# Norms and softplus of a two-block transformer kernel: half a square sum on VectorE, epsilon as a column, softplus on VectorE

## Chip, cores and metric

One core of a Trainium2 chip runs the whole program. The metric is the device time of one launch in microseconds (us). The engines are named as in the profile: PE is TensorE (its weight loads are PEld), DVE is VectorE, ACT is ScalarE, POOL is GpSimd, and SP issues the DMAs.

## What is computed

The input is 256 rows of width 1024, all in float32. A first block mixes a stick-breaking attention and a Mamba-2 (SSD) branch, then does a cross attention to a memory and a SwiGLU feed-forward. A second block has two layers: forget-gate attention ("fox") and latent attention ("mla"), each beside a small memory attention and followed by a convolutional feed-forward. Cut to what the change touches:

```
rms_norm(x, g) = x * rsqrt(mean(x*x, axis=-1) + 1e-6) * g        # rows of 1024, also q and k of each head (64 or 96)
dt             = softplus(dt_raw + dt_bias)                       # SSD: 2 x 32 heads per row
log_f          = log_sigmoid(f + b_f) = -softplus(-(f + b_f))     # fox: 12 heads per row
```

## The kernel before

The 256 rows are two tiles of 128 (t = 0 and t = 1), one row per partition. Every weight block of 128 x 1024 comes by DMA into `wr`. It is split into a high part `wh` (a rounding copy, by ACT or DVE) and a low part `wl` (the difference, by DVE or POOL). PE makes three products per block (high by high, low by high, high by low). These products are most of PE's work, and the splits are most of the work of ACT and DVE.

The program is written as some dozens of small generator threads (one per tile, per attention lane, per norm). A planner runs them first without the chip. `Engine` (L327) gives each operation an estimated cost, `Model` (L181 to L309) keeps the estimated time of every engine and buffer, and `next` (L480) picks the thread whose next operation can start first, with priorities and due times. `model_kernel` (L2231) plans once, then up to six times more with the order and the due times of the pass before, and emits the pass whose PE ends first in the model. So the order of every engine's queue comes from the estimated costs, and a changed operation can change the order of all that follows. Where a thread yields a list of operations, as for the copies of the weight split, the planner takes the engine on which it would end first. All operations are emitted through L363, so all have that line in the profile; matmuls have L652 and transposes L656.

The pieces that the change touches:

- `rms` (L828): the sum of squares of a row of 1024, as two halves. ACT squares each half with a running sum into one column (`accum_out`, in the trace an ACTIVATE and an ACTIVATION_READ_ACCUMULATOR), one half after the other, with one scratch of 512 columns. It runs 18 times: for both tiles of x, `mem` and `mem_2` (`inv_rms`, L862), before the cross attention, fox and mla (`prenorm`, L837), and before the three feed-forwards (`prenorm_joint`, L886). In `prenorm_joint` x is scaled by the result before it is transposed, so PE's transposes come after the norm; in `prenorm` the result is only applied to products.
- `rsqrt` (L682): two POOL steps. A TENSOR_SCALAR adds the two halves and epsilon, and a TENSOR_TENSOR raises to the power -1/2 (`mhalf`).
- `headnorm` (L1727): the same for the heads of a row. ACT squares n x d elements, DVE reduces them to n sums, POOL adds epsilon, POOL takes the power, DVE multiplies; then PE transposes the result (`heads_T`, `mem_q`). It runs 18 times: 12 times with 8 heads (fox: d = 64, mla: d = 96, three chunks and two tiles each) and 6 times with 4 heads.
- `softplus` (L995): exp on ACT, then a series in u/(2+u). Three of its steps are on DVE and 19 on POOL. It runs once for SSD's dt (128 x 64, called from `dt_part`, L1285) and once per tile for fox's gate (128 x 12, called from `fox_gate`, L1914). In `fox_gate` a product with a triangle of ones (`triu`) follows, whose result every q and k of that tile waits for.

Of the kernel before, what the change touches and what calls it, by code (L numbers as in the profile page):

```python
# [15 lines left out]
OP = mybir.AluOpType  # L16
AX = mybir.AxisListType.X

D = 1024
# [301 lines left out]
class Engine:  # L321
# [5 lines left out]
    def __getattr__(self, op):  # L327
# [3 lines left out]
        def call(*a, **k):  # L331
# [20 lines left out]
            else:  # L352
                port = bool(ins)
                c = 0.0023 * n + 0.25
                if k.get("op") == OP.pow:
                    c = 0.165 * n + 0.45
                elif op == "affine_select":
                    c = 0.00145 * n + 0.1
                elif op == "tensor_copy":
                    c = 0.001 * n + 0.19  # L360
                elif op == "memset":
                    c = 0.0009 * n + 0.07
# [17 lines left out]
class Program:  # L380
# [300 lines left out]

    def rsqrt(self, r, ms, more=None):  # L682

        n = r.shape[1]
        if more is None:
            yield self.G.tensor_scalar(ms, ms, EPS, None, op0=OP.add)
        else:
            yield self.G.tensor_scalar(ms, ms, more, EPS, op0=OP.add, op1=OP.add)
        yield self.G.tensor_tensor(r, ms, self.const["mhalf"][:, :n], op=OP.pow)

    def drop(self, key, users=2):
# [136 lines left out]
    def rms(self, src, r):  # L828

        junk = yield ("b", 512)  # L830
        m0, m1 = self.col(), self.col()
        for h, m in enumerate((m0, m1)):
            yield self.act(junk.ap, src[:, 512 * h:512 * h + 512], "Square", scale=1.0 / 32, accum_out=m)
        junk.free()
        yield from self.rsqrt(r, m0, m1)

# [117 lines left out]
    def postnorm(self, bs, x, name):  # L954
# [6 lines left out]
        junk.free()  # L961
        yield from self.rsqrt(r, m0, m1)
        y = yield ("b", D)
# [31 lines left out]
    def softplus(self, out, x, n):  # L995

        V, G = self.V, self.G
        w = yield ("b", n * 5)
        a, u, s, s2, q = (w.ap[:, i * n:(i + 1) * n] for i in range(5))
        yield V.scalar_tensor_tensor(a, x, -1.0, x, op0=OP.mult, op1=OP.max)  # L1000
        yield self.act(u, a, "Exp", scale=-1.0)
        yield G.tensor_scalar(s, u, 2.0, None, op0=OP.add)
        yield V.reciprocal(s, s)
        yield G.tensor_tensor(s, s, u, op=OP.mult)
        yield G.tensor_tensor(s2, s, s, op=OP.mult)
        yield G.tensor_scalar(q, s2, 1.0 / 15, None, op0=OP.mult)
        for m in (13, 11, 9, 7, 5, 3):
            yield G.tensor_scalar(q, q, 1.0 / m, None, op0=OP.add)
            yield G.tensor_tensor(q, q, s2, op=OP.mult)
        yield G.tensor_scalar(q, q, 1.0, 2.0, op0=OP.add, op1=OP.mult)  # L1010
        yield G.tensor_tensor(q, q, s, op=OP.mult)
        yield V.tensor_scalar(a, x, 0.0, None, op0=OP.max)
        yield G.tensor_tensor(out, q, a, op=OP.add)
        w.free()
# [712 lines left out]
    def headnorm(self, dst, src, n, d):  # L1727

        yield ("m", [n * d, 2 * n], [])
        junk = yield ("b", n * d)  # L1730
        s = yield ("b", 2 * n)
        ms, r = s.ap[:, :n], s.ap[:, n:2 * n]
        yield self.act(junk.v(n), src, "Square", scale=d ** -0.5)
        yield self.V.tensor_reduce(ms, junk.v(n), axis=AX, op=OP.add)
        junk.free()
        yield self.G.tensor_scalar(ms, ms, EPS, None, op0=OP.add)
        yield self.G.tensor_tensor(r, ms, self.const["mhalf"][:, :n], op=OP.pow)
        yield self.V.tensor_tensor(dst, src, r[:, :, None].to_broadcast([128, n, d]), op=OP.mult)
        s.free()
        yield ("r", dst)  # L1740
# [613 lines left out]
```

## Time and profile before

| | |
|---|---|
| time, median of 3 runs | 1309.0 us (1307.93 to 1310.06) |
| the profiled execution's own time | 1311.11 us |
| its span, first to last instruction | 1309.4 us |
| PE busy | 1281.2 us (98%), 8332 matmuls |
| PEld, DVE, ACT, POOL busy | 1142.1 (87%), 932.4 (71%), 810.7 (62%), 181.2 us (14%) |
| granted PE clock, mean | 0.995 |

The share of busy time is that of one execution. Matmuls overlap in the records, and their ends are modelled. So PE at 98% is no statement of peak speed; it says that there are few moments in which no matmul is under way.

### The profile page before, as it was taken

What the parts mean: (1) busy time and instruction counts of PE and PEld (TensorE: products, weight loads), DVE (VectorE), ACT (ScalarE), POOL (GpSimd) and SP (SyncE); (2) the same over time, 40 slices, a digit from 0 to 9 for tenths busy, and PEclk for the clock granted to TensorE, in tenths of its full rate; (3) what the DMA queues carried; (4) which work ended last, traced back from release to release, by engine and by line L of the source; (5) the groups of instructions that cost most, each with busy time, mean ns of one, the idle gap of its engine ahead of it and who ended that gap; (6) DMA issues with size and microseconds to landing.
All of it is one profiled execution on the core that took longest, in us unless ns stands there. A gap on an engine that the chain in (4) does not pass through costs nothing.

```text
span 1309.4 us, 21881 instructions
## 1 busy us (share of the span) xinstructions
PE 1281.2 (98%) x8332; PEld 1142.1 (87%) x8332; DVE 932.4 (71%) x1519; ACT 810.7 (62%) x1443; POOL 181.2 (14%) x324
## 2 busy tenths in 40 slices
PE   8999999999999999999999999899999999999998
PEld 6998998998888888999997888689999777799997
DVE  5766888988675737655447678788776788786774
ACT  6556678786745647544447656876554777865552
POOL 3053010022010002000004521000000332100000
PEclk9999999999999999999999999899999999999999
DMA  8723543455764715655564433476654333375540
GB/s 301 232 75 116 178 161 110 137 203 180 267 213 136 250 66 177 230 188 180 190 227 130 161 113 129 152 234 223 198 185 133 115 113 112 118 247 189 186 164 33
DMA packets 63322, 221.10 MB, mean 169 GB/s; under 512 B 7536, under 2 KB 7664, under 8 KB 63216
## 3 DMA queue, kind: packets, MB, share of 16 engines
q1 hardware_dynamic: 63216, 219.70, 50.2%
q8 instruction: 65, 1.06, 0.3%
q14 instruction: 41, 0.34, 0.1%
HBM read 218.62 MB, written 1.05 MB: 168 GB/s over the span
## 4 chain that ended last, share of the span: by engine, by line
PE 85%; DVE 6%; ACT 5%; DMA 2%; issue 1%; POOL 1%; SPq 0%; ACTq 0%; DVEq 0%; POOLq 0%
PE pa L652 82%; DVE arena L363 3%; PE pa L656 3%; ACT arena L363 3%; DVE wl L363 2%; DMA wr<-in_w_in 1%; ACT wh L363 1%; ACT L553 1%; DVE arena_r L363 1%; POOL small L363 1%; DMA arena<-in_mem 1%; DMA wr<-in_w_up 0%; ACT arena_r L363 0%; POOL arena L363 0%; SPq L660 0%
## 5 line engine op out<-in xcount | busy, mean ns | idle before, releaser
L363 DVE TENSOR_TENSOR wl<-wr,wh 128x1024 fp32r<-128x1024 f32 (+1 forms) x395 | 472.6, 1212 | 178.4 <-ACT wh L363 172.9
L652 PE MATMUL pa<-wh,arena_r 128*128 128x512 f32 (+2 forms) x1812 | 588.2, 394 | 5.1 <-ACT wh L363 3.4
L363 ACT ACTIVATE wh<-wr 128x1024 fp32r<-128x1024 f32 (+2 forms) x393 | 406.6, 1044 | 268.6 <-PE pa L652 187.3
L652 PE MATMUL pa<-arena_r,wh 128*128 128x256 f32 (+2 forms) x2736 | 495.6, 283 | 0.0
L652 PEld LDWEIGHTS pa<-arena_r,wh 128*128 128x128 f32 (+2 forms) x2736 | 425.8, 190 | 4.6 <-issue 1.1
L652 PEld LDWEIGHTS pa<-wh,arena_r 128*128 128x128 f32 x1812 | 340.9, 189 | 76.1 <-ACT wh L363 4.2
L652 PE MATMUL pa<-arena_r,wl 128*128 128x256 f32 (+2 forms) x1368 | 385.6, 282 | 0.0
L652 PE MATMUL pa<-wl,arena_r 128*128 128x512 f32 (+2 forms) x906 | 352.6, 389 | 2.9 <-DVE wl L363 2.9
L652 PEld LDWEIGHTS pa<-arena_r,wl 128*128 128x128 f32 (+2 forms) x1368 | 260.1, 190 | 0.2
L652 PEld LDWEIGHTS pa<-wl,arena_r 128*128 128x128 f32 x906 | 171.6, 189 | 33.9 <-DVE wl L363 3.9
L363 ACT ACTIVATE arena<-arena 128x512 f32<-128x512 f32 (+6 forms) x130 | 80.3, 628 | 31.1 <-DVE arena L363 27.8
L652 PE MATMUL pa<-arena 128*64 128x128 f32 (+4 forms) x888 | 92.5, 288 | 3.2 <-ACT arena L363 2.4
L652 PEld LDWEIGHTS pa<-arena 128*64 128x64 f32 (+3 forms) x888 | 78.0, 161 | 18.4 <-issue 7.0
L363 ACT ACTIVATE arena<-pa 128x512 f32<-128x512 f32 (+4 forms) x98 | 53.6, 555 | 63.6 <-PE pa L652 38.3
L363 POOL TENSOR_SCALAR small<-small 128x1 f32<-128x1 f32 x38 | 15.2, 401 | 494.6 <-ACT arena L363 342.3
L363 DVE TENSOR_TENSOR arena<-arena 128x512 f32<-128x512 f32 (+4 forms) x117 | 68.2, 601 | 13.3 <-POOL arena L363 5.9
L656 PE MATMUL pa<-ident,arena 128*128 128x128 f32 (+3 forms) x446 | 66.6, 281 | 9.6 <-DVE arena L363 7.0
L363 DVE SCALAR_TENSOR_TENSOR arena<-pa,cols,arena 128x255 f32<-128x255 f32 (+1 forms) x136 | 57.7, 476 | 25.6 <-ACT arena L363 24.3
L656 PEld LDWEIGHTS pa<-ident,arena 128*128 128x128 f32 (+3 forms) x446 | 52.7, 139 | 23.3 <-DVE arena L363 10.4
L363 ACT ACTIVATE arena<-pa,small 128x128 f32<-128x128 f32 (+2 forms) x147 | 55.5, 453 | 24.8 <-PE pa L652 24.1
L363 DVE TENSOR_TENSOR arena<-pa,arena 128x512 f32<-128x512 f32 (+3 forms) x74 | 48.9, 670 | 29.1 <-PE pa L652 24.3
L363 DVE SCALAR_TENSOR_TENSOR arena<-arena,cols 128x128 f32<-128x128 f32 (+3 forms) x152 | 59.0, 422 | 6.6 <-ACT arena L363 4.8
(128 smaller groups left out, 777.1 us busy)
## 6 DMA issues: line engine op xcount, KB each, us to landing
wr<-in_w_up SPq DMA_DIRECT2D x96, 512.0 KB, 4.1
wr<-in_w_in SPq DMA_DIRECT2D x80, 512.0 KB, 4.4
wr<-in_w_gu SPq DMA_DIRECT2D x44, 512.0 KB, 4.2
wr<-in_w_dn SPq DMA_DIRECT2D x44, 512.0 KB, 4.7
wr<-in_w_down SPq DMA_DIRECT2D x22, 512.0 KB, 3.6
wr<-in_w_fox SPq DMA_DIRECT2D x20, 512.0 KB, 3.6
wr<-in_w_br_ssm SPq DMA_DIRECT2D x16, 512.0 KB, 4.2
wr<-in_w_xkv SPq DMA_DIRECT2D x16, 512.0 KB, 3.7
```

The lines of the kernel that those rows point to most:

```text
L363: emit = (lambda: f(*a, **k)) if f else (lambda: None)
L553: self.real.preload_act_table_set(s)
L652: self.T.matmul(out, l, r, start=start, stop=stop, skip_group_check=True)
L656: self.T.transpose(out, in_, self.const["ident"][:k, :k])
```

## The change

- `rms`: the second half of the squares may run on DVE (a scalar_tensor_tensor with a running sum); the planner picks ACT or DVE. Where the arena has room, the two halves write to different scratch columns.
- `rsqrt`: it can leave out the epsilon step; with two halves, they swap their places as operands.
- `headnorm`: POOL first writes epsilon to one more column per head, DVE's reduction sums it in, and POOL's step that added it is gone.
- `softplus`: all steps but exp are on DVE, with add and multiply fused: 15 DVE steps and the exp.
- In the cost estimates a power given as second operation is priced as one; no operation of the kernel has that.

```diff
-    def rsqrt(self, r, ms, more=None):
+    def rsqrt(self, r, ms, more=None, eps=True):
-        if more is None:
+        if more is not None:
+            yield self.G.tensor_scalar(ms, ms, more, EPS, op0=OP.add, op1=OP.add)
+        elif eps:
             yield self.G.tensor_scalar(ms, ms, EPS, None, op0=OP.add)
-        else:
-            yield self.G.tensor_scalar(ms, ms, more, EPS, op0=OP.add, op1=OP.add)
         yield self.G.tensor_tensor(r, ms, self.const["mhalf"][:, :n], op=OP.pow)
+    def sumsq(self, junk, src, m, both=False):
+        o = [self.act(junk, src, "Square", scale=1.0 / 32, accum_out=m)]
+        if both:
+            o.append(self.V.scalar_tensor_tensor(junk, src, 1.0 / 1024, src, op0=OP.mult, op1=OP.mult, accum_out=m))
+        return o
 def rms
-        junk = yield ("b", 512)
+        two = self.mem.fits([D])
+        junk = yield ("b", D if two else 512)
-        for h, m in enumerate((m0, m1)):
-            yield self.act(junk.ap, src[:, 512 * h:512 * h + 512], "Square", scale=1.0 / 32, accum_out=m)
+        yield self.sumsq(junk.ap[:, :512], src[:, :512], m0)
+        yield self.sumsq(junk.ap[:, 512 * two:512 * two + 512], src[:, 512:], m1, True)
-        yield from self.rsqrt(r, m0, m1)
+        yield from self.rsqrt(r, m1, m0)
 def softplus (every G below was or becomes V; w, a, u, s, s2, q as before)
-        yield G.tensor_scalar(s, u, 2.0, None, op0=OP.add)
+        yield V.tensor_scalar(s, u, 2.0, None, op0=OP.add)
         yield V.reciprocal(s, s)
-        yield G.tensor_tensor(s, s, u, op=OP.mult)
-        yield G.tensor_tensor(s2, s, s, op=OP.mult)
-        yield G.tensor_scalar(q, s2, 1.0 / 15, None, op0=OP.mult)
+        yield V.tensor_tensor(s, s, u, op=OP.mult)
+        yield V.tensor_tensor(s2, s, s, op=OP.mult)
+        yield V.tensor_scalar(q, s2, 1.0 / 15, None, op0=OP.mult)
         for m in (13, 11, 9, 7, 5, 3):
-            yield G.tensor_scalar(q, q, 1.0 / m, None, op0=OP.add)
-            yield G.tensor_tensor(q, q, s2, op=OP.mult)
-        yield G.tensor_scalar(q, q, 1.0, 2.0, op0=OP.add, op1=OP.mult)
-        yield G.tensor_tensor(q, q, s, op=OP.mult)
+            yield V.scalar_tensor_tensor(q, q, 1.0 / m, s2, op0=OP.add, op1=OP.mult)
+        yield V.scalar_tensor_tensor(q, q, 1.0, s, op0=OP.add, op1=OP.mult)
         yield V.tensor_scalar(a, x, 0.0, None, op0=OP.max)
-        yield G.tensor_tensor(out, q, a, op=OP.add)
+        yield V.scalar_tensor_tensor(out, q, 2.0, a, op0=OP.mult, op1=OP.add)
 def headnorm
-        yield ("m", [n * d, 2 * n], [])
-        junk = yield ("b", n * d)
+        yield ("m", [n * (d + 1), 2 * n], [])
+        junk = yield ("b", n * (d + 1))
+        sq = junk.v(n)
+        yield self.G.memset(sq[:, :, d:], EPS)
-        yield self.act(junk.v(n), src, "Square", scale=d ** -0.5)
-        yield self.V.tensor_reduce(ms, junk.v(n), axis=AX, op=OP.add)
+        yield self.act(sq[:, :, :d], src, "Square", scale=d ** -0.5)
+        yield self.V.tensor_reduce(ms, sq, axis=AX, op=OP.add)
-        yield self.G.tensor_scalar(ms, ms, EPS, None, op0=OP.add)
-        yield self.G.tensor_tensor(r, ms, self.const["mhalf"][:, :n], op=OP.pow)
+        yield from self.rsqrt(r, ms, eps=False)
```

## Rows read from the trace of the kernel before

**Rows 1.** Busy time by stretch: us, then PE, PEld, DVE, ACT, POOL, clock, DMA.
```profile
60.00:155.00 95.00, 94.97 (x720) 87.19 (x719) 68.35 (x100) 58.90 (x94) 33.41 (x48) 1.00 0.36 120
824.00:850.00 26.00, 21.57 (x89) 17.08 (x88) 22.32 (x47) 23.10 (x44) 1.46 (x6) 0.87 0.54 182
1060.00:1100.00 40.00, 36.98 (x239) 30.18 (x237) 33.27 (x81) 30.20 (x79) 11.10 (x20) 0.96 0.32 106
```
**Rows 2.** Waits of PE: who waited for whom, us in total, times, longest.
```profile
PE pa L656 <- DVE arena L363: 7.0, 7, 3.4
...
PE pa L652 <- POOL small L363: 1.9, 2, 1.2
```
**Rows 3.** Timeline, 705 to 720, fox's softplus of t = 0 on POOL.
```profile
706.65 0.67 POOL L363 TENSOR_SCALAR arena<-arena 128x12 f32<-128x12 f32 x1 [2.42 <-ACT arena L363]
...
709.22 1.11 POOL L363 TENSOR_SCALAR arena<-arena 128x12 f32<-128x12 f32 x1
...
718.00 0.77 POOL L363 TENSOR_TENSOR small<-arena 128x12 f32<-128x12 f32 x1 [0.54 <-DVE arena L363]
```
**Rows 4.** Timeline of PE, 715 to 720.
```profile
718.83 0.39 PE L652 MATMUL pa<-small,triu 128*128 128x12 f32 x2 [1.20 <-POOL small L363]
```
**Rows 5.** DVE's groups by shape: busy us, mean ns, idle before.
```profile
L363 DVE SCALAR_TENSOR_TENSOR arena<-pa,small,arena 128x512 f32<-128x512 f32 x24 | 17.5, 743 | 16.1 <-POOL small L363 13.3 <-PE pa L652 2.7
...
L363 DVE TENSOR_REDUCE arena<-arena 128x128 f32<-128x512 f32 x8 | 8.5, 1083 | 1.0 <-ACT arena L363 0.9
...
L363 DVE TENSOR_SCALAR arena<-arena 128x12 f32<-128x12 f32 x4 | 0.7, 172 | 0.1
...
L363 DVE RECIPROCAL arena<-arena 128x12 f32<-128x12 f32 x2 | 0.5, 228 | 1.5 <-POOL arena L363 1.5
...
L363 DVE SCALAR_TENSOR_TENSOR arena<-arena 128x12 f32<-128x12 f32 x2 | 0.3, 166 | 0.0
```
**Rows 6.** POOL's groups by shape, headnorm's epsilon step and a small fill.
```profile
L363 POOL TENSOR_SCALAR arena<-arena 128x8 f32<-128x8 f32 x12 | 4.5, 375 | 50.1 <-DVE arena L363 49.9
...
L363 POOL MEMSET arena<- 128x4 f32 x12 | 1.2, 104 | 0.1
```
**Rows 7.** Timeline, 1087 to 1097, one headnorm of mla: POOL, DVE, PE.
```profile
1088.33 0.24 POOL L363 TENSOR_SCALAR arena<-arena 128x8 f32<-128x8 f32 x1 [2.85 <-DVE arena L363]
1088.66 1.66 POOL L363 TENSOR_TENSOR arena<-arena,mhalf 128x8 f32<-128x8 f32 x1
...
1090.72 0.97 DVE L363 TENSOR_TENSOR arena<-arena 128x768 f32<-128x768 f32 x1
...
1091.75 3.20 PE L656 MATMUL pa<-ident,arena 128*96 128x128 f32 x16 [1.83 <-DVE arena L363]
```
**Rows 8.** Timeline, 838 to 845, the norm before the first convolutional feed-forward.
```profile
839.99 1.28 DVE L363 TENSOR_TENSOR arena<-pa,arena 128x512 f32<-128x512 f32 x2
...
841.18 1.13 DVE L363 SCALAR_TENSOR_TENSOR arena<-arena,cols 128x128 f32<-128x128 f32 x4
...
841.46 0.63 ACT L363 ACTIVATE arena<-arena 128x512 f32<-128x512 f32 x1
841.99 0.19 ACT L363 ACTIVATION_READ_ACCUMULATOR arena<-arena 128x1 f32 x1
...
842.28 0.30 POOL L363 TENSOR_SCALAR small<-small 128x1 f32<-128x1 f32 x1 [7.37 <-ACT arena L363]
...
843.85 1.54 PE L656 MATMUL pa<-ident,arena 128*128 128x128 f32 x6 [3.41 <-DVE arena L363]
```
**Rows 9.** Busy time and clock in short stretches (columns as in the first group).
```profile
844.00:846.00 2.00, 2.00 (x9) 1.95 (x10) 2.00 (x6) 1.94 (x6) 0.00 (x0) 0.50 0.00 0
...
850.00:852.00 2.00, 2.00 (x11) 1.64 (x10) 1.93 (x6) 0.50 (x3) 0.53 (x1) 1.00 0.69 262
...
1092.00:1096.00 4.00, 3.91 (x24) 3.21 (x22) 4.00 (x11) 3.25 (x7) 0.00 (x0) 0.57 0.10 20
```
**Rows 10.** Timeline, 1118 to 1132, the norm before the last feed-forward.
```profile
1125.41 1.22 DVE L363 TENSOR_TENSOR wl<-wr,wh 128x1024 fp32r<-128x1024 f32 x1
...
1128.07 1.10 PE L656 MATMUL pa<-ident,arena 128*128 128x128 f32 x8 [0.46 <-DVE arena L363]
```

More of the change, by code (lines that the diff above doesn't have):

```diff
@@ L354, in call @@
                 c = 0.0023 * n + 0.25
-                if k.get("op") == OP.pow:
+                if OP.pow in (k.get("op"), k.get("op1")):
                     c = 0.165 * n + 0.45
@@ L961, in postnorm @@
         junk.free()
-        yield from self.rsqrt(r, m0, m1)
+        yield from self.rsqrt(r, m1, m0)
         y = yield ("b", D)
@@ L995, in softplus @@
     def softplus(self, out, x, n):
-        V, G = self.V, self.G
+        V = self.V
         w = yield ("b", n * 5)
```

## The prediction

> **What bounds the kernel now.** I read the page first (PE busy 98% of the span), then the busy time by stretch, PE's waits, and the timelines around those waits. By stretch the reader sees that PE is full nearly everywhere: from 60 to 155 it is busy 94.97 of 95.00 us, although GpSimd works through the long softplus of dt there [rows 1]. Only few stretches are loose, among them 824 to 850 (21.57 of 26 us busy) and 1060 to 1100 (36.98 of 40), and there the mean granted clock is below 1.00, at 0.87 and 0.96 [rows 1]. So the path is PE's own work, and an edit is worth only what it takes from a wait of PE. Two kinds of wait belong to this change [rows 2]: transposes that wait for VectorE (7.0 us in 7 waits, the longest 3.4), which are mostly transposes of normalised data, and products that wait for a small column from GpSimd (1.9 us in 2). All the rest of the norms and of softplus lies beside matmuls and costs nothing now.
>
> **Softplus.** It takes 19 GpSimd steps away per call, so 57 in three calls, and adds 12 VectorE steps per call, 36 in all. In fox, t = 0, the GpSimd chain runs from 706.65 to 718.77 [rows 3], and the product with the triangle waits 1.20 us for its last step [rows 4]. Much of the chain is not arithmetic: the same kind of step takes 1.11 us at 709.22 [rows 3], while the mean of the group of the next width is 375 ns [rows 6]. On VectorE a step of that width takes 166 to 172 ns and the reciprocal, which is there already, 228 [rows 5]. 12 x 0.17 + 0.23 = 2.3 us if nothing comes between. VectorE is in order and shared with the weight splits of about 1.2 us each [rows 10]; even with four of them between, the chain ends near 706.7 + 2.3 + 4.9 = 713.9, some 4.8 us ahead of 718.77. So the 1.20 us go: **-1.2 us**. What is late next are headnorms of the same chunk, which the second edit shortens. The limits: 0, if the next item in PE's queue was late as well, and -1.9, if the second of the two waits goes too. The call of t = 1 and that of dt give nothing: dt's lies in the full stretch 60 to 155 [rows 1]. The cover for the added 36 x 0.17 = 6.1 us of VectorE work is that VectorE is not the bound in these stretches (68.35 of 95 us busy in the first [rows 1]). Without that cover a part of the 6.1 us would stand between a weight split and its matmul.
>
> **Epsilon as a column.** It removes 18 GpSimd steps, each on the chain reduce, epsilon, power, multiply, transpose. At 1088.33 the step takes 0.24 us and the power follows at 1088.66, so 0.33 us go per headnorm [rows 7]. Added are 18 fills of 4 or 8 columns, 0.10 us each [rows 6], issued ahead of the squares; and the reduction gets one element more per head. What is queued behind a fill on GpSimd are other norms' powers; a fill that waits for its scratch would hold these. On the path I count three of the 7 transposes' waits of [rows 2] and the second wait for GpSimd's column, because in each a headnorm's power ended shortly before (this count is an estimate from the timelines; one of the four stands in the rows): 4 x 0.33 = **-1.3 us**. The clearest is the wait of 1.83 us at 1091.75, where the multiply of 0.97 us starts at 1090.72, 0.40 after the power's end [rows 7]. That slack also shows why the limits are wide: from -2.6 (twice the count, if a chunk's chain is late at each attention group) to +0.7 (a fill that waits for its scratch and holds two powers back, by a step's 0.33 each).
>
> **Half a square sum on VectorE.** Where both halves are ready at once it would save a whole ACT pass with its read-out. But behind a residual add they are not. At 839.99 two adds take 1.28 us together and end at 841.27; ACT's second square starts at 841.46, its read-out ends at 842.18 and GpSimd goes on at 842.28 [rows 8]. That is 1.01 us from the second add to GpSimd. A scalar_tensor_tensor of 512 columns without a sum takes 743 ns [rows 5]; with the same 0.10 us of hand-over it is 0.84, so the gain is 0.17 us. Two waits of PE end with such a norm, 3.41 us at 843.85 [rows 8] and 0.46 at 1128.07 [rows 10]: 2 x 0.17 = **-0.35 us**. No row shows VectorE with a running sum over a row. From below I take the 743 ns; from above the slowest VectorE pass over 512 elements, a strided reduction of 1083 ns [rows 5], which would turn the gain into a loss of 0.17 per norm, +0.35. I take 743, the row with the same operation and width. The other norms lie beside matmuls.
>
> A page of the Trainium skill speaks against this edit: Vector Engine (DVE) Microarchitecture Reference, section 7, "Points that are easy to get wrong", says that a scalar-tensor-tensor with two non-bf16 sources in SBUF runs at half the throughput, because no read port is left for the accumulator. By that rule the sum of the three edits would be -1.3 instead of -2.85, as worked out from rows under the third rival. No row has this form with a sum, so the trace neither bears it out nor denies it.
>
> The sum is -1.2 - 1.3 - 0.35 = -2.85 us. The profiled execution took 1311.11 us, its span 1309.4; it would come to 1308.3. The median of the runs is 1309.0, 2.1 below that execution, so the forecast is **1306.1 us**. Its own range, from the limits above, is 1304.3 to 1308.5.
>
> **Rivals.**
>
> *The clock comes back as well.* After the waits of 3.41 and 1.83 us the granted clock is 0.50 from 844 to 846 and 0.57 from 1092 to 1096 [rows 9], which is the lower level of 1.2 GHz. The mean clock of 0.87 over 26 us means 6.8 us at half, and 0.96 over 40 us means 3.2 us at half [rows 1]; about 0.75 us of the first pass before PE starts again. Half of the rest is lost, 3.0 and 1.6 us. Shorter waits may leave the clock up; for it speaks that the changed chains end exactly in these two waits, against it that the first shrinks by only 0.17 us. With the larger one back: 1306.1 - 3.0 = 1303.1 us.
>
> *The gains do not arrive.* Removing one release of PE shows the next. The transposes of several waits also need a free PSUM bank, and VectorE's multiply before 1091.75 started 0.40 us after the power [rows 7], so it was held by VectorE's own queue. Then only a few tenths remain: 1309.0 us, less or more by 1.
>
> *VectorE with a sum is slow.* If the running sum makes VectorE pass over its input at half the pace, the step takes 2 x 743 = 1486 ns [rows 5], and GpSimd goes on 1.59 us after the second add instead of 1.01 [rows 8]: 0.58 lost at each of the two norms, 1309.0 - 1.2 - 1.3 + 1.2 = 1307.7 us. Against it speaks only that a plain step with two inputs shows no such pace; no row has the sum. This is the page's rule from above.
>
> *Slower: the second square waits in VectorE's queue.* The order comes from the planner's estimates. If VectorE gets the square behind other work, the norm ends later than on ACT; that begins when it starts over 0.17 us after the second add. At 841.18 four convolution steps of 1.13 us follow the adds [rows 8], and at 1125.41 a weight split of 1.22 [rows 10]. Behind the four steps the square would start at 842.31, end at 843.05, and GpSimd would go on at 843.15 for 842.28: 0.87 us later. Behind the norm are the scaling, then the transposes, then all products of the feed-forward. Two norms cost +1.7 us, and the wait at 1128 may then grow long enough to lower the clock, at the 3.0 us of the first rival: +4.7, of which softplus pays back 1.2: 1312.5 us. Against it: the planner compares the ends on both engines before it chooses.
>
> **How the numbers follow.** Forecast 0.38, clock back 0.22, gains do not arrive 0.17, slow sum 0.05, slower 0.18. A change under 0.2% (2.6 us) can't be told from none here, so faster means under 1306.4 and slower over 1311.6. Somewhat over half of the forecast's own range is under 1306.4 (0.23), with the clock's case 0.45. Slower are its own case and a little of the redrawn order, 0.20. The rest, 0.35, is the same. The range goes from 1301.5 (both clock stretches back) to 1312.5.
>
> **What would show it.** In the profile after: softplus's last step for t = 0 on VectorE, several us ahead of its triangle product, with no wait of PE for it; the powers of headnorm straight after the reduction, 0.3 us earlier, and fills of 0.1 us that wait for nothing; squares on VectorE of about 0.75 us that start right after the second add; GpSimd's busy time lower by more than 20 us (57 steps of softplus and 18 of epsilon at 0.33 would be 25), and ACT's lower as well; PE's idle time smaller by 2 to 3 us, with no more than two stretches at half clock. Wrong it is if PE's busy stretches themselves shift in length, if a third stretch at half clock appears, or if the squares stand behind weight splits on VectorE.

## The result, and the profile after

The changed kernel takes 1318.75 us (median of 4, 1316.51 to 1320.85) against 1308.56 (median of 4). The ratio is 1.0066, with an interval of 1.0052 to 1.0080: slower, where a gain of 2.9 us was forecast, and outside the range of 1301.5 to 1312.5. The profiled execution took 1320.23 us, its span 1318.5, 9.1 more than before.

The page's busy times:

```profile
span 1318.5 us, 21894 instructions
...
PE 1282.7 (97%) x8332; PEld 1143.4 (87%) x8332; DVE 945.0 (72%) x1570; ACT 803.9 (61%) x1421; POOL 169.9 (13%) x272
```

PE has 1.5 us more of work and 7.6 us more of idle time. GpSimd's busy time fell by 11.3 us only, where the prediction had looked for over 20. The waits of PE (waiter, releaser: us in total, times, longest):

```profile
PE pa L656 <- DVE arena L363: 15.5, 11, 5.0
PE pa L652 <- ACT arena L363: 4.4, 8, 0.8
PE pa L652 <- ACT wh L363: 2.6, 1, 2.6
```

The first row was 7.0 in 7 waits [rows 2]. It grew by 8.5 us, all waits of PE together by 7.2. Of the 8.5 us, 1.6 came at the wait of 850.73, 2.2 at 1136.36, 1.2 at 500.59, and 2.3 in mla from 1038 on, where four waits of 0.76 to 1.74 us stand for three before. The waits for GpSimd's column are gone, as forecast. Busy time by stretch, columns as in [rows 1]:

```profile
824.00:850.00 26.00, 21.02 (x105) 16.94 (x103) 20.36 (x36) 20.61 (x34) 4.02 (x5) 1.00 0.53 180
...
850.00:854.00 4.00, 3.27 (x12) 2.59 (x13) 3.66 (x12) 2.11 (x9) 1.46 (x4) 0.57 0.37 131
...
1138.00:1142.00 4.00, 4.00 (x13) 2.79 (x12) 3.13 (x12) 2.98 (x8) 0.00 (x0) 0.71 0.40 131
...
60.00:155.00 95.00, 95.00 (x723) 87.56 (x723) 70.86 (x116) 60.20 (x94) 24.69 (x28) 1.00 0.38 128
```

The full stretch stayed full. Near 850 the norm before the convolutional feed-forward still has the longest wait, and the lower clock still follows it (0.57 over 850 to 854, as in [rows 9]). Stretches with the lower clock also stand near 297 (0.56 from 297 to 299), 1048 (0.77 from 1046 to 1050) and 1138, where the kernel before has only that of 1092 to 1096 besides; both have one more near the start (before: 0.56 from 10 to 12). So the third stretch, which the prediction named as a sign against itself, is there. The timeline near 850 answers to [rows 8]; ahead of it stand the end of softplus, for [rows 3, 4], and an earlier norm:

```profile
497.87 2.39 POOL L363 TENSOR_TENSOR wl<-wr,wh 128x1024 fp32r<-128x1024 f32 x1
497.93 2.60 DVE L363 TENSOR_SCALAR arena<-arena,small 128x512 f32<-128x512 f32 x1 [1.16 <-POOL small L363]
...
718.08 0.17 DVE L363 SCALAR_TENSOR_TENSOR small<-arena 128x12 f32<-128x12 f32 x1
719.68 0.29 PE L652 MATMUL pa<-small,triu 128*128 128x12 f32 x2
...
844.62 1.37 DVE L363 TENSOR_TENSOR arena<-pa,arena 128x512 f32<-128x512 f32 x2
...
846.24 0.68 DVE L363 SCALAR_TENSOR_TENSOR arena<-arena 128x512 f32<-128x512 f32 x1
846.86 0.08 DVE L363 DVE_READ_ACCUMULATOR arena<-arena 128x1 f32 x1
...
847.12 0.31 POOL L363 TENSOR_SCALAR small<-small 128x1 f32<-128x1 f32 x1 [11.24 <-DVE arena L363]
...
847.50 0.58 POOL L363 TENSOR_TENSOR small<-small,mhalf 128x1 f32<-128x1 f32 x1
848.05 2.35 POOL L363 TENSOR_TENSOR wl<-wr,wh 128x1024 fp32r<-128x1024 f32 x1
848.12 2.96 DVE L363 TENSOR_SCALAR arena<-arena,small 128x512 f32<-128x512 f32 x2 [1.18 <-POOL small L363]
...
850.73 1.97 PE L656 MATMUL pa<-ident,arena 128*128 128x128 f32 x8 [5.03 <-DVE arena L363]
```

Softplus's last step is done 1.4 us ahead of its product (718.25, 719.68), which waits for nothing. The square on VectorE takes 0.68 us. But it does not start right after the second add, which ends at 845.99: a step of 0.41 us at 845.91 stands between, and GpSimd goes on 1.13 us after that add, where it was 1.01 [rows 8]. So the norm gains nothing by it. Then, right after the power, GpSimd starts a weight split, and the two scaling steps on VectorE, 0.49 us each by the mean of their group before, take 2.96 us. PE's transposes start once the first of them is done, after 5.03 us where it was 3.41 [rows 8]. At 497.93 the same pattern holds one scaling step for 2.60 us, and makes a wait of 1.16 us at 500.59 that was not there. The last norm, which answers to [rows 10], has both squares on ACT and no split in its way:

```profile
1133.07 0.60 PE L656 MATMUL pa<-ident,arena 128*128 128x128 f32 x4
...
1133.32 0.63 ACT L363 ACTIVATE arena<-arena 128x512 f32<-128x512 f32 x1 [0.75 <-DVE arena L363]
...
1134.00 0.63 ACT L363 ACTIVATE arena<-arena 128x512 f32<-128x512 f32 x1
...
1135.82 0.49 DVE L363 TENSOR_SCALAR arena<-arena,small 128x512 f32<-128x512 f32 x1 [1.26 <-POOL small L363]
...
1136.36 1.48 PE L656 MATMUL pa<-ident,arena 128*128 128x128 f32 x8 [2.69 <-DVE arena L363]
```

Nothing in this norm is slower than before, yet PE waits 2.69 us. Before, four other transposes ran while the norm was under way:

```profile
1126.94 0.66 PE L656 MATMUL pa<-ident,arena 128*128 128x128 f32 x4 [0.89 <-ACT arena L363]
```

With the 0.46 us behind them [rows 10] PE was idle for 1.35 us there. Now four such transposes run at 1133.07, before the first square starts, and PE has nothing left to do. No term of the prediction could show this: the order itself is another one.

The powers of the head norms do start straight after the reduction, as forecast (at 1050.73, 0.08 us after it). But PE still waits 1.74 us at 1053.53 for the multiply behind.

The groups of VectorE and GpSimd by shape (busy us, mean ns, idle before), first two rows of the kernel before, then the changed one:

```profile
L363 DVE TENSOR_SCALAR arena<-arena,small 128x512 f32<-128x512 f32 x7 | 3.2, 487 | 3.2 <-POOL small L363 3.2
...
L363 POOL TENSOR_TENSOR wl<-wr,wh 128x1024 fp32r<-128x1024 f32 x11 | 29.4, 2675 | 113.6 <-ACT wh L363 111.2 <-PE pa L652 2.5
```

```profile
L363 DVE TENSOR_SCALAR arena<-arena,small 128x512 f32<-128x512 f32 x7 | 7.5, 1082 | 5.5 <-POOL small L363 5.5
L363 DVE SCALAR_TENSOR_TENSOR arena<-arena 128x512 f32<-128x512 f32 x7 | 4.8, 683 | 2.0 <-DMA arena<-in_mem 1.9
...
L363 POOL TENSOR_TENSOR wl<-wr,wh 128x1024 fp32r<-128x1024 f32 x15 | 38.9, 2597 | 137.9 <-ACT wh L363 137.9
...
L363 POOL MEMSET arena<- 128x8 f32 x17 | 1.8, 110 | 16.2 <-DVE arena L363 9.7 <-PE pa L652 6.4
```

The 9.5 us more of weight splits on GpSimd, and a half-sized one of 1.3, are why GpSimd did not fall by 20. Only 7 of the 18 norms have a square on VectorE. The fills cost what [rows 6] said. Six small fills wait for their scratch, against the prediction's sign, but behind each the next step of GpSimd waits again for its own input, 0.55 us at the least, so they held nothing back.

### The profile page after: what moved, and what is told of

Its sections match the earlier page's. It is cut to its first block, busy times and chain, and to the rows that moved or that the text cites. A ratio compares the mean times of both kernels' runs of the same rounds, so it can differ in the third digit from the quotient of the medians.

```text
span 1318.5 us, 21894 instructions
## 1 busy us (share of the span) xinstructions
PE 1282.7 (97%) x8332; PEld 1143.4 (87%) x8332; DVE 945.0 (72%) x1570; ACT 803.9 (61%) x1421; POOL 169.9 (13%) x272
## 3 DMA queue, kind: packets, MB, share of 16 engines
HBM read 218.62 MB, written 1.05 MB: 167 GB/s over the span
## 4 chain that ended last, share of the span: by engine, by line
PE 86%; DVE 5%; ACT 4%; DMA 3%; issue 1%; POOL 0%; SPq 0%; ACTq 0%; DVEq 0%; POOLq 0%
PE pa L652 83%; DVE arena L363 4%; PE pa L656 3%; DMA wr<-in_w_in 2%; ACT arena L363 2%; DVE wl L363 1%; ACT wh L363 1%; DMA wr<-in_w_down 0%; ACT arena_r L363 0%; DMA wr<-in_w_br_ssm 0%; ACT L553 0%; DVE arena_r L363 0%; POOL small L363 0%; POOL arena L363 0%; SPq L660 0%
## 5 line engine op out<-in xcount | busy, mean ns | idle before, releaser
L363 DVE TENSOR_TENSOR wl<-wr,wh 128x1024 fp32r<-128x1024 f32 (+2 forms) x390 | 468.4, 1218 | 171.8 <-ACT wh L363 167.6
L363 ACT ACTIVATE wh<-wr 128x1024 fp32r<-128x1024 f32 (+2 forms) x397 | 412.0, 1045 | 282.5 <-PE pa L652 206.6
L363 ACT ACTIVATE arena<-arena 128x512 f32<-128x512 f32 (+5 forms) x123 | 76.1, 631 | 26.3 <-DVE arena L363 19.8
L363 ACT ACTIVATE arena<-pa 128x512 f32<-128x512 f32 (+4 forms) x91 | 49.8, 554 | 60.3 <-PE pa L652 43.3
L656 PE MATMUL pa<-ident,arena 128*128 128x128 f32 (+3 forms) x446 | 66.8, 281 | 17.6 <-DVE arena L363 15.5
L363 DVE TENSOR_TENSOR arena<-arena 128x512 f32<-128x512 f32 (+5 forms) x123 | 69.4, 581 | 13.1 <-POOL arena L363 6.9
L363 ACT ACTIVATE arena<-pa,small 128x128 f32<-128x128 f32 (+5 forms) x144 | 54.4, 450 | 24.2 <-PE pa L652 23.4
```

Source lines behind the costliest of these rows:

```text
L363: emit = (lambda: f(*a, **k)) if f else (lambda: None)
L656: self.T.transpose(out, in_, self.const["ident"][:k, :k])
```

## The experiments

The expectations set theory T1 (the newly drawn order costs; the edits themselves do little) against T2 (the edits cost wherever they stand). Ratios are to the kernel before in the same batch, whose medians were 1308.6 to 1310.4. "Waits" is the sum of all waits of PE in the profile. "Clock" is the span times one minus the mean granted clock, an estimate, from clocks rounded to 0.001, of what the lower level takes.

| kernel | order of | time | ratio, interval | span | waits | clock |
|---|---|---|---|---|---|---|
| before | before | 1308.56 | 1 | 1309.4 | 24.4 | 6.5 |
| after | after | 1318.75 | 1.0066, 1.0052 to 1.0080 | 1318.5 | 31.6 | 9.2 |
| before_order_new_steps | before | 1314.75 | 1.0038, 1.0025 to 1.0050 | 1312.9 | 27.6 | 9.2 |
| before_order_half_only | before | 1314.27 | 1.0035, 1.0022 to 1.0048 | 1311.0 | 28.9 | 3.9 |
| before_order_softplus_eps | before | 1308.39 | 0.9996, 0.9987 to 1.0004 | 1305.1 | 22.9 | 5.2 |
| before_order_softplus_early | before | 1310.08 | 0.9999, 0.9988 to 1.0009 | 1308.1 | 24.7 | 5.2 |
| before_order_seven_squares | before | 1311.52 | 1.0012, 1.0003 to 1.0021 | 1308.5 | 25.3 | 5.2 |
| new_order_old_steps | after | 1333.27 | 1.0181, 1.0162 to 1.0201 | 1330.3 | 41.2 | 14.6 |
| split_in_pieces | after | 1317.08 | 1.0062, 1.0049 to 1.0076 | 1314.0 | 29.0 | 9.2 |
| old_steps_third_pass | drawn afresh | 1325.02 | 1.0119, 1.0105 to 1.0133 | 1324.8 | 34.5 | 13.2 |
| old_steps_due_weight | drawn afresh | 1334.91 | 1.0193, 1.0179 to 1.0207 | 1333.2 | 37.5 | 20.0 |
| old_steps_12_passes | drawn afresh | 1318.36 | 1.0065, 1.0053 to 1.0078 | 1314.8 | 28.7 | 10.5 |
| softplus_new_order | drawn afresh | 1322.42 | 1.0091, 1.0075 to 1.0106 | 1321.4 | 32.1 | 14.5 |
| softplus_eps_new_order | drawn afresh | 1320.44 | 1.0084, 1.0066 to 1.0103 | 1318.3 | 31.4 | 11.9 |
| new_steps_other_order | drawn afresh | 1324.23 | 1.0112, 1.0098 to 1.0126 | 1321.5 | 35.0 | 13.2 |
| new_steps_ranked_best | drawn afresh | 1311.57 | 1.0013, 1.0004 to 1.0022 | 1309.0 | 25.7 | 6.5 |
| new_steps_16_passes | drawn afresh | 1315.80 | 1.0046, 1.0033 to 1.0058 | 1312.6 | 26.7 | 11.8 |
| new_steps_high_cap | drawn afresh | 1314.53 | 1.0045, 1.0032 to 1.0058 | 1312.7 | 28.0 | 10.5 |

Span less waits less clock is 1273.3 to 1278.5 in every row, though the spans lie 28 us apart. So most of what differs from kernel to kernel is how long PE waits and how long it then runs at the lower clock; up to 5 us of it is not in these two. Before to after this is 7.2 + 2.7 = 9.9 of waits and clock for a span 9.1 longer. These are single executions. The clock column's estimate from all executions on record is 10.9 us for the changed kernel (mean of 4) and 4.7 to 5.7 for the one before (means of 9 to 23), so the lower clock is a larger part of the loss than the two profiles say, about half of it.

**The edits without a new order.** The planner sees the steps of before and draws its order; when an operation is emitted, the new step stands in for the old one:

```diff
-        yield G.tensor_tensor(s2, s, s, op=OP.mult)
+        yield self.via(G.tensor_tensor(s2, s, s, op=OP.mult), lambda: R.tensor_tensor(s2, s, s, op=OP.mult))   # R: VectorE
+            self.via(o, lambda m=m: self.V.real.scalar_tensor_tensor(...))   # second square, all 18 norms
-        yield self.G.tensor_scalar(ms, ms, EPS, None, op0=OP.add)            # headnorm
+        yield self.via(self.G.tensor_scalar(ms, ms, EPS, None, op0=OP.add))  # emits nothing
```

Expected of `before_order_new_steps`: 

> The planner sees the steps of the kernel before and makes its order; only what is emitted in their places is new: softplus on VectorE, the second half of all 18 square sums on VectorE, headnorm's epsilon step gone (epsilon is left out there, without a fill in its place). PE's order is that of the kernel before, step by step. Theory 1 (the order that the planner drew costs the 10 us, not the edits): 1304 to 1309 us, the gains that the prediction summed or a part of them. Rival (the edits themselves cost, by second squares and softplus steps that wait in VectorE's queue): 1313 us or more.

1314.75: this is the rival's number, not T1's. With all 18 squares on VectorE the edits do cost, so I took them apart.

Expected of `before_order_half_only`: 

> The drawn order of the kernel before, on all engines; the one edit is that the second half of the sum of squares of all 18 norms runs on VectorE in the place where ScalarE's stood (the kernel as changed does this in 7 norms). Softplus and the head norm's epsilon stay as before. The run with all three edits in this order came to +4.4 us. Theory A (an edit that the order was not drawn for costs, because the second square stands in VectorE's queue behind work that was placed there for other reasons): 1312 to 1315, and the waits of the transposes for VectorE's arena tile grow from 7.0 us to over 10. Theory B (the +4.4 came from softplus's steps standing where GpSimd's stood): 1307 to 1310, transposes' wait about 7 us.

Expected of `before_order_softplus_eps`: 

> The drawn order of the kernel before; the edits are softplus in 12 VectorE steps, each at the place of the GpSimd step that it replaces, and the head norm without the step that adds epsilon (left out, so the norm of a zero row would differ). All squares stay on ScalarE. Prediction's sum for these two alone: 1.2 + 1.3 = 2.5 us less, 1306 to 1308. Theory A (the +4.4 us is the second square's): 1306 to 1309. Theory B (softplus's steps where GpSimd's stood hold VectorE's queue): 1312 to 1315.

Theory A in both: the second square alone makes 1314.27, with 10.6 us of transposes' waits, and softplus and epsilon alone 1308.39, which can't be told from before. How a square that is quicker on VectorE costs time is seen at the norm of [rows 10] (timeline of the kernel with the squares only):

```profile
1126.08 1.21 DVE L363 TENSOR_TENSOR wl<-wr,wh 128x1024 fp32r<-128x1024 f32 x1
...
1127.21 0.68 DVE L849 SCALAR_TENSOR_TENSOR arena<-arena 128x512 f32<-128x512 f32 x1
...
1129.63 1.09 PE L656 MATMUL pa<-ident,arena 128*128 128x128 f32 x8 [1.50 <-DVE arena L363]
```

The adds before the norm end at 1126.16. The square then waits for a weight split and starts at 1127.21, and PE's wait is 1.50 us for 0.46. That is the mechanism of the prediction's slower rival, at the split that it named. At four other places of this run PE's wait is longer than before by 0.7 to 1.0 us; one of them, at 1096.78, is as long in the kernels of this order without that square.

In the kernel with softplus and epsilon alone, two timelines show why the forecast gains do not come:

```profile
716.52 0.16 DVE L1034 SCALAR_TENSOR_TENSOR small<-arena 128x12 f32<-128x12 f32 x1
716.73 0.39 PE L652 MATMUL pa<-small,triu 128*128 128x12 f32 x2 [1.28 <-DVE small L1034]
...
1084.75 1.64 POOL L363 TENSOR_TENSOR arena<-arena,mhalf 128x8 f32<-128x8 f32 x1 [2.85 <-DVE arena L363]
...
1087.07 0.15 DVE L363 RECIPROCAL arena<-arena 128x2 f32<-128x2 f32 x1
1087.15 0.94 DVE L363 TENSOR_TENSOR arena<-arena 128x768 f32<-128x768 f32 x1
...
1088.14 1.08 PE L656 MATMUL pa<-ident,arena 128*96 128x128 f32 x8 [1.79 <-DVE arena L363]
```

Softplus's steps stand in VectorE's queue at the places planned for GpSimd, so its last one is as late as before, and the product waits 1.28 us. In the head norm the epsilon step is gone, but the power ends at 1086.39 and the multiply starts at 1087.15, straight after a reciprocal of the attention that stands ahead of it in VectorE's queue. The wait is 1.79 us for 1.83 [rows 7]. The wait for GpSimd's column that the prediction counted, 0.66 us at 1032.26 before, is 0.66 here too; it is now ACT that ends it.

**Softplus in one go, in the order of before.** All 12 steps are emitted at the place of the first one:

```diff
-        yield self.via(G.tensor_scalar(s, u, 2.0, None, op0=OP.add), lambda: R.tensor_scalar(s, u, 2.0, None, op0=OP.add))
+        yield self.via(G.tensor_scalar(s, u, 2.0, None, op0=OP.add), chain)   # all 12 steps
```

Expected of `before_order_softplus_early`: 

> The drawn order of the kernel before, epsilon left out of the head norm, and the 12 VectorE steps of softplus written together at the place of the first GpSimd step, where they stood at the 12 places of the steps that they replace. The wait of 1.3 us for softplus's product that this order still showed goes if it came from those places. If the prediction's term for softplus holds (the wait is the gain): 1.2 us under 1308.39, so 1306.5 to 1307.7. If the steps only push VectorE's other work back by their 2 us: 1308.5 to 1311, with a new wait on VectorE near 718.

```profile
707.73 0.17 DVE L1016 TENSOR_SCALAR arena<-arena 128x12 f32<-128x12 f32 x1
...
710.34 0.17 DVE L1025 SCALAR_TENSOR_TENSOR small<-arena 128x12 f32<-128x12 f32 x1
...
718.09 0.28 PE L652 MATMUL pa<-small,triu 128*128 128x12 f32 x2
...
719.55 0.29 PE L652 MATMUL pa<-arena_r,wh 128*12 128x128 f32 x2 [0.51 <-DVE arena_r L363]
...
733.21 0.50 PE L652 MATMUL pa<-wl,arena_r 128*128 128x512 f32 x1 [0.57 <-DVE wl L363]
```

The chain takes 2.78 us instead of 12, it ends 7.6 us ahead of the product, and the product waits for nothing. Behind it PE now waits 0.51 us for a tile of VectorE and 0.57 for a weight split there; neither wait stands in before or in the kernel with the steps spread out. The ratio is 0.9999: the wait was turned into two others. The second expectation held, not the one of the prediction's term.

**The whole change without a new order.** As the first kernel, with the second square on VectorE only in the seven norms where the changed kernel has it:

```diff
-            if h:
+            if h and (self.cur.key, turn) in ON_VECTOR:
```

Expected of `before_order_seven_squares`: 

> The drawn order of the kernel before, on all engines, with all three edits, and the second square on VectorE in just the seven norms in which the changed kernel has it there (the head norm's epsilon is left out, so the norm of a zero row would differ). Softplus and epsilon alone came to 1308.39, with all 18 squares moved to 1314.75. Theory T1 (the edits cost little without a new order; what costs is the new order): 1308 to 1311. Rival T2 (the edits that the changed kernel really makes cost 10 us in any order): 1316 to 1319.

1311.52, ratio 1.0012. T1's upper end is missed by 0.5 us, T2's lower end by 4.5. The change as made costs about 1.6 us in the order of before (0.0012 of 1309) and 8.6 in its own (0.0066). The 7 us between are the new order's, which includes where each weight split runs. The fills are only in the changed kernel; the next run has none, and nearly the same waits of the transposes.

**The new order without the edits.** The planner sees the new steps, and the old ones are emitted in their places:

```diff
+        self.via(V.tensor_tensor(s2, s, s, op=OP.mult), lambda: R.tensor_tensor(s2, s, s, op=OP.mult))   # R: GpSimd
```

Expected of `new_order_old_steps`: 

> The other way round: the planner sees the new steps and makes the order of the changed kernel, but in their places the old ones are emitted (softplus on GpSimd, all squares on ACT, an epsilon step before each power). PE's order is that of the changed kernel. Theory 1 (order): 1316 us or more, as slow as the changed kernel or 1 to 4 us slower. Rival (edits): 1307 to 1312 us.

1333.27, 14.5 us over the changed kernel, where T1 had looked for 1 to 4. Its waits of PE:

```profile
PE pa L656 <- DVE arena L363: 15.7, 11, 5.2
PE pa L652 <- DVE small L363: 4.5, 1, 4.5
```

```profile
81.23 4.61 DVE L363 TENSOR_TENSOR small<-small,nega 128x32 f32<-128x32 f32 x2 [4.84 <-POOL small L1041]
```

The first row is that of the changed kernel, 15.5 in 11: these waits belong to the order, not to the steps. The second is the product behind dt's softplus, at 85.89, in a stretch that was full in both kernels [rows 1]. The chain on GpSimd ends at 81.19, and the two multiplies behind it on VectorE take 4.61 us beside two weight splits on GpSimd (81.15 to 85.78), where the changed kernel has them done in 0.47 at 76.90. So steps for which an order was not drawn cost here too. The new steps are worth 14.5 us in their order, and in the other they cost 1.6; a price of an edit without its order has no meaning in this kernel.

**Other orders for the old steps.** One constant of the planner is changed:

```diff
-PASSES = 6
+PASSES = 3                              # old_steps_third_pass
-DUE, DMIN, DMAX = 0.02, -15.0, 10.0
+DUE, DMIN, DMAX = 0.019, -15.0, 10.0    # old_steps_due_weight
```

Expected of `old_steps_third_pass`: 

> The kernel before with three planner passes after the first instead of six: same steps, another order. Theory 1 says that any other order of this planner is some us away from the one that the tuned kernel has: 1312 to 1322 us. Rival: within 3 us of 1309, for no step has changed.

Expected of `old_steps_due_weight`: 

> The kernel before with the planner's weight of due times at 0.019 instead of 0.02: same steps, another order, and by the planner's own ranking a worse one than with three passes. Theory 1: 1314 to 1325 us, slower than the run with three passes. Rival: within 3 us of 1309.

1325.02 and 1334.91, 3 and 10 us above what T1 had looked for, with not one operation changed. (Which engine a weight split runs on is part of the order: the first of these has 14 and a half-sized one on GpSimd, where before has 11.) A redrawn order alone costs 15 and 25 us.

**One edit or two, with an order drawn for them** (squares all on ScalarE, whose edit against the changed kernel is shown; then the kernel before with softplus's edit only):

```diff
-        yield self.sumsq(junk.ap[:, 512 * two:512 * two + 512], src[:, 512:], m1, True)
+        yield self.sumsq(junk.ap[:, 512 * two:512 * two + 512], src[:, 512:], m1)
```

Expected of `softplus_eps_new_order`: 

> The changed kernel with all squares on ScalarE, so softplus and epsilon alone, and the planner draws its order afresh. In the order of before these two came to 1308.39. Theory T1 (a new order costs, whatever the edit): 1313 to 1335, with the waits of the transposes for VectorE's arena tile above 9 us. Rival T3 (the choice of an engine for the second square is what spoils the order): 1306 to 1310.

Expected of `softplus_new_order`: 

> The kernel before with softplus's edit alone, and the planner draws its order afresh. Theory T1: 1313 to 1335, another time than with epsilon too. Rival T3 (without the second square's choice the order stays as good): 1306 to 1310.

1320.44 and 1322.42. The first is the kernel that came to 1308.39 in the order of before, so 12 us are the order's. The two can't be told apart. The sign in the waits that was expected of the first held in the second only (15.6 us for VectorE's arena tile); in the first that row is 6.7, and PE waits for other tiles instead, 31.4 us in all.

**Weight splits in quarters**, every engine's sequence as in the changed kernel:

```diff
+            P = [slice(n * j, n * j + n) for j in range(4)]
+            o[1].emit = lambda: [self.G.real.tensor_tensor(L[:, p], raw[:, p], H[:, p].bitcast(F32), op=OP.subtract) for p in P]
```

Expected of `split_in_pieces`: 

> The changed kernel and its order, every engine's sequence the same, but each weight split on GpSimd (15 of 128x1024 and one of 128x512) is written as four instructions of a quarter each. Theory P (a VectorE step that reads SBUF waits until the GpSimd instruction that it met ends, so the normalisation at 848.12 took 2.96 us for two steps and the one at 497.93 2.60 us for one): these steps fall to 1.2 us or less each, the wait for the transposes at 850.73 falls from 5.03 us to under 4, the group of 7 such steps falls from a mean of 1082 ns to under 800, and the time falls by 2 to 5 us, to 1314 to 1317. Rival Q (VectorE and GpSimd share the port step by step, so both slow down whatever the instruction's length): the normalisations stay above 2 us, time 1317 to 1321.

```profile
493.75 0.96 DVE L363 TENSOR_SCALAR arena<-arena,small 128x512 f32<-128x512 f32 x1 [1.16 <-POOL small L363]
...
841.82 3.34 POOL L612 TENSOR_TENSOR wl<-wr,wh 128x256 fp32r<-128x256 f32 x4
...
841.89 1.81 DVE L363 TENSOR_SCALAR arena<-arena,small 128x512 f32<-128x512 f32 x2 [1.18 <-POOL small L363]
...
842.89 0.66 PE L660 MATMUL pa<-ident,arena 128*128 128x128 f32 x4 [3.41 <-DVE arena L363]
...
843.63 0.94 DVE L363 TENSOR_TENSOR arena_r<-arena,arena_r 128x256 fp32r<-128x256 f32 x1
...
846.67 1.22 PE L656 MATMUL pa<-wh,arena_r 128*128 128x512 f32 x2 [1.73 <-DVE arena_r L363]
...
L363 DVE TENSOR_SCALAR arena<-arena,small 128x512 f32<-128x512 f32 x7 | 4.7, 685 | 5.5 <-POOL small L363 5.5
...
L612 POOL TENSOR_TENSOR wl<-wr,wh 128x256 fp32r<-128x256 f32 x60 | 50.7, 878 | 137.0 <-ACT wh L363 137.0
```

Theory P: with shorter instructions on GpSimd the same two steps take 1.81 us for 2.96, the one of the earlier norm 0.96 for 2.60, the group's mean falls from 1082 to 685 ns, and the wait from 5.03 to 3.41. VectorE's step ended only after the instruction that it met on GpSimd had ended. The Trainium skill says this of the two engines, in SBUF — State Buffer, section "Who interferes with whom": they share a pair of ports, by an exclusive lock and not by sharing the rate. The trace agrees, 2.96 us beside one long instruction and 1.81 beside four short ones. The time, 1317.08, lies 1.7 us under the changed kernel's, just outside what P had looked for, and the intervals of the ratios overlap, so a gain in time is not shown. Nor does this run price the splits: their quarters hold the steps behind the norm instead (0.94 us at 843.63 for a step that takes 0.41 in the changed kernel), and at 846.67 PE waits 1.73 us that it did not wait there. How much of the loss comes from the splits stays open.

**Other orders for the new steps.**

```diff
-DUE, DMIN, DMAX = 0.02, -15.0, 10.0
+DUE, DMIN, DMAX = 0.02, -15.0, 10.5     # new_steps_other_order; 11.0 in new_steps_high_cap
-PASSES = 6
+PASSES = 8                              # new_steps_ranked_best, with DUE 0.019; 16 and 0.018 in new_steps_16_passes
```

Expected of `new_steps_other_order`: 

> All three edits as in the changed kernel; one constant of the planner (the cap of a due time, 10 to 10.5) differs, so that it draws another order. Theory T1 (the time is set by which order is drawn, the same steps spread over 15 to 25 us): it differs from the changed kernel's 1318.75 by more than 3 us, either way; its best draw by the planner's own ranking would be under 1312. Rival T2 (the edits themselves cost 10 us wherever they are placed): within 3 us of 1318.75.

Expected of `new_steps_ranked_best`: 

> The changed kernel with two constants of the planner altered (weight of a due time 0.02 to 0.019, 8 passes for 6): it keeps a pass that the planner ranks ahead of all other orders here, the one of before among them. If the ranking tells (theory R): 1300 to 1308, the waits of TensorE well under the 31.6 us of the changed kernel. If the order is a lottery (theory L): 1315 to 1335.

Expected of `new_steps_16_passes`: 

> The changed kernel with the weight 0.018 and 16 passes: a third order for the same steps, ranked just ahead of the one of before. Theory R: 1303 to 1311. Theory L: 1315 to 1335.

Expected of `new_steps_high_cap`: 

> The changed kernel with the cap of a due time at 11 for 10: a fourth order for the same steps, ranked just ahead of the one of before. Theory R: 1303 to 1311. Theory L: 1315 to 1335.

The same steps run from 1311.57 to 1324.23, so T1 held in new_steps_other_order: 5.5 us away, with nothing changed but the order. The order that the planner's model ends earliest is the best of them, and it takes back 7.2 of the 10.2 us lost; its waits:

```profile
PE pa L656 <- DVE arena L363: 11.3, 11, 3.4
PE pa L652 <- ACT arena L363: 7.8, 12, 1.2
```

But neither theory's numbers fit. R wanted 1300 to 1308 from the best, and L at least 1315 from all; the three ranked ahead lie at 1311.57 and 1314.53, between the two, and at 1315.80, just within L's. new_steps_other_order, which the planner also ranks ahead of the changed kernel's order, is 5.5 us slower than that. The last kernel of this kind, 12 passes for the old steps, keeps a pass that the planner ranks slightly ahead of the order of before:

Expected of `old_steps_12_passes`: 

> The kernel before with 12 passes for 6: it keeps the eleventh, which the planner ranks slightly ahead of the one of before. Theory R: 1305 to 1310. Theory L: 1315 to 1335.

1318.36, 8.5 us slower than the order it was ranked ahead of. So the ranking tells something among the new steps, and misses by 5 to 9 us between single orders. In numbers, PE ends in the planner's own model (`model_kernel`, which needs no chip) at 1287.9 us for the kernel before and 1293.6 for the changed one. It ends at 1282.1, 1285.5, 1285.1 and 1289.7 for ranked_best, high_cap, 16_passes and other_order, and at 1286.2 for old_steps_12_passes. Of the eleven orders run, that of the kernel before is the fastest. No version here beats it beyond its uncertainty; before_order_softplus_eps equals it.

## Why the prediction was wrong

The step that failed is the sum, "-1.2 - 1.3 - 0.35 = -2.85 us". All its terms are taken from waits that stand in the trace of before, so it holds only if every queue keeps its order. But a planner draws the order from the estimated costs, so a change of steps draws a new one. The prediction gave this "a little of the redrawn order" in its chance for slower and no price. It was the largest term: about +7 us of the 8.6 to 10.2, as the seven squares in the order of before show (1.0012 against 1.0066). Taken the other way round, order first, the redraw is +24 us (1.0181) and the steps give 14.5 back; either way it is the term that was left out. The planner's redrawing was known before; two orders for the old steps, 15 and 25 us slower, are what its price looks like. A first price was also to be had from the planner itself, whose model ends PE 5.8 us later in the changed kernel's order.

Term by term, in the order of before:

- Softplus, -1.2: the chain's length was right (2.78 us by itself for 2.3 worked out), and in the changed kernel the product waits for nothing. The gain was not: with the wait gone, VectorE's pushed-back steps give PE two new ones of 0.51 and 0.57. The prediction had looked for what is late next among the head norms; it was a tile and a weight split from VectorE's own queue. The cover that it named for the added 6.1 us of VectorE's work did not hold at this place.
- Epsilon, -1.3: the wait at 1091.75 went from 1.83 to 1.79. The prediction saw that the multiply started 0.40 after the power and used it to widen a limit; it was the sign that the power did not set the wait. Where the releasing step starts later than its input is ready, only its queue is worth shortening. The factor of 4 was too high in itself: of the seven transposes' waits, besides those of [rows 8, 10], two are of 0.16 us and one of 0.28, so that not every counted one could give 0.33. Softplus and epsilon together came to 0.9996 of before.
- Half square, -0.35: the step takes 0.68 us and 0.08 for its sum, about what the row of 743 ns said. The start was wrong: at the one of the two norms that got it, another step stood between, and GpSimd went on 0.12 us later than before and not 0.17 earlier. The rule of the Trainium skill that the prediction weighed (Vector Engine (DVE) Microarchitecture Reference, section 7, "Points that are easy to get wrong") would have halved its pace, 1.49 us; the trace does not agree, at 0.68 us in the groups of 7 and of 18 such steps, which read one tile as both sources. But its price is a place in VectorE's queue: all 18 cost 4.6 us (1.0035), the seven that the planner chose about 2.1 (1.0012 less 0.9996).

Of the rivals, the slower one had the mechanism right, at the split before the last feed-forward that it named: in before_order_half_only the square starts 1.05 us after the adds and PE waits 1.04 longer. In the changed kernel the planner left that square on ACT, so this is not where its time went. "Gains do not arrive" is what softplus and epsilon did. The clock went the other way: 2.7 us more at the lower level by the table, and 5 to 6 by all executions.

The range "from the limits above", 1304.3 to 1308.5, does not follow from them either: added up they give 1304.15 to 1310.05.

What the prediction did not have at all is GpSimd's weight splits. Four more and a half-sized one went there, and two of them start right behind a norm's power, which accounts for the wait at 850.73 (+1.6) and for that at 500.59 (1.16). It is tempting to say that they went there because softplus and epsilon left GpSimd room, but the runs speak against it: old_steps_third_pass, with all the old steps on GpSimd, has 14 and a half-sized one there, softplus_eps_new_order has 12, and new_steps_ranked_best has 15 and costs 1.7 us. Their number goes with the drawn order, and where they stand decides.

Open: why the order of before is so good. Its waits are short and its mean clock high, but no single place explains it, and the planner's model does not tell it from orders 9 us slower. Measured, it ends 21 us after the model's end, and the other ten orders 25 to 37.

## What to carry to other kernels

Where a planner or scheduler draws the order from estimated costs, price an edit in two parts: in the fixed order, and the redraw. A first estimate of the second is the scheduler's own end before and after, where it has one; here that was 5.8 us later. The price itself is measured by nudging a constant that changes no step; if that alone moves the time by 10 us, a local gain of 3 us predicts nothing, and the order should be frozen while the edit is tried. In the fixed order, take a gain only where the releasing instruction starts as soon as its input is there, and price a step moved to a busy in-order engine by what stands around it in the queue, not by its own duration.

## What the hardware showed that was not expected

- A VectorE step of 128x512 with a per-row scalar took 2.60 us beside one GpSimd tensor_tensor of 128x1024, and 0.96 beside the same work in quarters (0.49 alone). The quarters cost GpSimd more, 4 x 878 ns for 2597. Steps that read PSUM were not held: beside the split of 188.40 to 191.75 in the changed kernel, five of 128x128 took 0.34 or 0.35 us each, 0.34 elsewhere. It goes the other way too: that split itself met a VectorE weight split and took 3.36 us, the one at 61.11, which met steps that read PSUM, 2.36.
- A running sum on VectorE costs 0.08 us, the row DVE_READ_ACCUMULATOR, on a pass of 0.68 us; the pass of the same width without one, which reads PSUM, takes 0.74 [rows 5].
